# A two-layer hybrid decoder trunk on one core: the first layer's input loaded a second time by tokens, its loads put in order of use, products on ones while they run, and the feed-forward norm computed per token

## The chip, the core and the metric

The kernel runs on one core of a Trainium2 chip. TensorE (PE; its weight loads are listed as PEld) multiplies 128x128 stationary blocks with moving blocks of up to 512 columns into PSUM. VectorE (DVE), ScalarE (ACT) and GpSimd (POOL) do the elementwise work; SyncE (SP) and ACT issue DMAs. The metric is the device time in microseconds, the median of several runs; lower is better.

## The reference

```
def rmsnorm(x, g):
    y = xf * lax.rsqrt(jnp.mean(xf * xf, axis=-1, keepdims=True) + NORM_EPS)
    return (y * g.astype(jnp.float32)).astype(x.dtype)

def hybrid_layer(x, ...):
    h = rmsnorm(x, g_mix)
    z = h @ w_in                       # 1024 -> 2884 columns, split among the mixers
    y_a = short_conv_mixer(...)        # gated convolution, 3 taps
    y_b = gmlp_mixer(...)              # layernorm, 128x128 lower-triangular mixing
    y_c = dsa_mixer(...)               # rotary; indexer scores, top 128 keys, softmax
    y_d = conformer_conv_mixer(...)    # 31 taps, layernorm, silu
    x = x + jnp.concatenate([y_a, y_b, y_c, y_d], axis=-1) @ w_out
    hf = rmsnorm(x, g_ffn)
    return x + (jax.nn.silu(hf @ w_gate) * (hf @ w_up)) @ w_down
```

There are 512 tokens, a width of 1024, two such layers, a hidden width of 2816, and a last rmsnorm. Everything is float32.

## The kernel before

Channels lie on the 128 partitions and tokens along the row: x is eight tiles `X[k]` of 128x512. A float32 product is made from three products of two parts each: every operand is split into a rounded part (`hi`, fp32r, a cast on ACT) and the rest (`lo`, a subtraction on DVE or, for the weight units in `POOL_LO`, on POOL); `mm3` issues hi\*hi, hi\*lo and lo\*hi. Weights come in units of 128x1024 floats (512 KB) through three buffers `wr`; their halves go to four buffers each of `wh` and `wl`, or, for the units in `DEEP`, to the 68 general buffers `u`. A unit is 24 products of 512 columns (`unit`); its sum stands in one of three PSUM banks `mm` (a fourth, `cv`, is shared with the convolution).

A norm is not applied to x. The products run on x times its gain (`prep`, two instructions on ACT and DVE and a third for the squares), and the factor 1/rms of each token is multiplied in when a PSUM bank is read. So products can start before the norm's factor is known, but a bank can't be read and given free before it is.

Each layer: `proj("qi", 0)` (indexer queries), `proj("kw", 0)` (indexer keys and weights), then the other 21 input units, rotary, scores, the top-k search (`MAX8`, `MATCH_REPLACE8` on DVE), convolution taps on DVE (the first `TAPS[i]` of 31; the rest on ACT and POOL), attention, the output projection, and the feed-forward part. There, units alternate gate and up (`pgt`, `pu`); the gate's bank is multiplied by `R`, the row of factors, and only then is it free.

How the factors are made, in three places:

- First layer: `square_sum` squares each `X[k]` on ACT and sums over its partitions with four products of two columns on `ones` per tile (a stationary block of squares, `ones` moving), 32 in all, before any result; then `bank_rsqrt` on a 128x4 tile and `spread`, four products with the identity that put the factors of the four blocks of tokens across all partitions.
- Second layer and last norm: `square` adds up squares on POOL and DVE; `col_rsqrt` makes four products of two columns at the end; then the same.
- Feed-forward: `wide_rsqrt` (L638): sums by two products with `ones_r` that leave the sum in every partition, and then scale, reciprocal, square root and one Newton step on whole 128x512 tiles.

The order of instructions on every engine is made by a list scheduler in the program (`Program.order`). It has a planned cost per operation, a due time worked back from the end (`STRETCH`, `HURRY`), boosts per part of a layer (`BOOST`), a plan of TensorE's clock (`clock`) and of the DMA bus, and writes the instructions out in the planned order; on the chip each engine runs its list in that order and waits where it must. A change of one number or operation can so move instructions anywhere.

Of the kernel before, what the change touches and what calls it, by code (L numbers as in the profile page):

```python
# [113 lines left out]
class Op:  # L114
    __slots__ = ("eng", "cost", "lat", "fn", "tiles", "preds", "succs", "table", "late", "wait",
                 "ready", "main", "i", "dma", "start", "key", "boost", "desc", "port")
# [7 lines left out]
class Program:  # L124
# [15 lines left out]
    def add(self, eng, cost, fn, outs, ins, lat=LAT, table=None, main=False, dma=0.0,  # L140
            port=False):
        o = Op()
        o.port = port
# [24 lines left out]
    def order(self):  # L168
# [43 lines left out]
        table, bus, port, out, done = None, 0.0, 0.0, [], 0  # L212
        while done < len(ops):
# [65 lines left out]
            if e == "PE":  # L279
                end = self.clock(o.start, o.cost)  # L280
# [25 lines left out]
    def clock(self, start, cost):  # L306
# [7 lines left out]
        self.busy += self.slow * cost  # L314
        return start + self.slow * cost
# [6 lines left out]
    def mm(self, out, l, r, start, stop, main=False):  # L322
# [5 lines left out]
                 [out.tile.view], [l, r], lat=0.2, main=main)  # L328

# [24 lines left out]
    def tr(self, out, x, ident):  # L354
        self.add("PE", 0.109, lambda: self.nc.tensor.transpose(out.ap(), x.ap(), ident.ap()),
                 [out], [x, ident], lat=0.2)

# [80 lines left out]
HURRY = 1.19  # L438
# [5 lines left out]
    {"rope": -2.0, "conv": 19.0, "a": -4.0, "z": 2.0, "s": 12.0, "g": 6.0, "topk": -3.0, "att": 27.0, "out": -6.0},  # L444
    {"rope": 2.0, "conv": 26.0, "a": -1.0, "z": 0.0, "s": 6.0, "g": 0.0, "topk": 5.0, "att": 2.0, "out": 0.0},
]
DEEP = (4, 5, 6, 7, 9, 10, 11, 12, 13, 15, 23, 25, 31)
HALVED = (0,)
TAPS = (20, 20)
POOL_LO = (3, 5, 7, 10, 11, 12, 20, 21, 22, 23, 24, 25, 29, 30, 31, 32)  # L450
# [27 lines left out]
def _record(pg, nc, a, o, cst, sml):  # L478
# [24 lines left out]


    stream, gate = [0], []

    def weights():
# [48 lines left out]
    ones_r = const("ones_r", 128, F32R)  # L556
# [14 lines left out]
    def square_sum(k):  # L571

        sq = U()
        if k == 0:
            acc["pt"] = SM()
        pg.act(sq, X[k], AF.Square)
        for t in range(4):
            pg.mm(acc["pt"][:, 2 * t:2 * t + 2], sq[:, t * 128:(t + 1) * 128], ones[:, :2],
                  k == 0 and t == 0, k == KT - 1 and t == 3)

# [9 lines left out]
    def prep(k, l, col, sums=square):  # L590
# [4 lines left out]
        sums(k)  # L595
# [30 lines left out]
    def col_rsqrt(ss, scale, eps):  # L626
# [11 lines left out]
    def wide_rsqrt(ss, scale, eps):  # L638

        hi, lo, ms, r, y, t, R = U(F32R), U(F32R), U(), U(), U(), U(), U()  # L640
        split(ss, hi, lo)
        pt = SM()
        pg.mm(pt, ones_r, hi, True, False)
        pg.mm(pt, ones_r, lo, False, True)
        pg.ts(ms, pt, scale, eps, ALU.mult, ALU.add)
        recip(r, ms)
        pg.act(y, r, AF.Sqrt)
        pg.stt(t, y, -0.5, y, ALU.mult, ALU.mult)
        pg.tt(t, t, ms, ALU.mult)
        pg.stt(R, t, 1.5, y, ALU.add, ALU.mult)  # L650
        return R
# [10 lines left out]
    def layer(l, xg):  # L662
# [26 lines left out]
        def raw_of(pt):  # L689
# [3 lines left out]
            return pt, sw  # L693
# [5 lines left out]
        first = raw_of(first)  # L699
# [271 lines left out]
        R = wide_rsqrt(acc["ss"], 1.0 / D, 1e-6)  # L971
# [56 lines left out]
    pg.dma(prm[0], a["prm"][0])  # L1028
    for k in range(KT):
        pg.dma(X[k], a["x"][:, k], eng="ACT" if k % 2 else "SP")  # L1030
# [6 lines left out]
    pg.act(ones_r, ones)  # L1037
# [3 lines left out]
    xg = [prep(k, 0, P_GM, square_sum) for k in range(KT)]  # L1041
# [96 lines left out]
```

## Time and profile before

| | |
|---|---|
| runs | 1196.33 us median of 3 (1193.57 to 1197.22) |
| profiled execution | 1194.45 us, its span 1192.6 us |
| PE busy | 1156.8 us, 5278 instructions |
| DVE, ACT, POOL busy | 639.2, 483.8, 312.8 us |

The span runs from the first to the last instruction of the program; 1.85 us lie around it. A busy PE includes products that run at half the clock or are spaced out, so the number of products in a stretch says more than the busy time.

### The profile page before, as it was taken

The numbers are of one execution on the slowest core, as the hardware profiler recorded it, in microseconds if no ns is written. First come the engines' busy times: TensorE is split into PE (matmuls) and PEld (weight loads), VectorE is DVE, ScalarE is ACT, GpSimd is POOL, SyncE is SP. The second block draws the span as 40 slices with busy tenths as digits, with TensorE's granted clock in tenths as the row PEclk, the third lists the DMA queues.
The fourth block names the chain that finished last, engine by engine and source line by source line (L and its number), as shares of the span: only waits on it lengthen the run. The fifth ranks groups of instructions, "written<-read, shape, count | busy, mean of one in ns | idle before, by whom it ended". The sixth has DMA issues, their size and how long they took to land.

```text
span 1192.6 us, 13996 instructions
## 1 busy us (share of the span) xinstructions
PE 1156.8 (97%) x5278; PEld 942.5 (79%) x5278; DVE 639.2 (54%) x1126; ACT 483.8 (41%) x769; POOL 312.8 (26%) x236
## 2 busy tenths in 40 slices
PE   7999989989999999999999999998999999999996
PEld 7777867868888888888877788787888888888886
DVE  3589997754343434333257999868343434332222
ACT  6464558543333333232244563766232323222221
POOL 3516762311111111010044568323111111110001
PEclk9999999989999999999999999999999999999998
DMA  6630122222322232332255002222223232323322
GB/s 225 196 105 19 44 85 84 71 71 91 103 90 104 89 105 86 97 115 96 81 184 167 27 27 89 72 89 88 70 89 105 90 102 93 102 84 98 98 63 70
DMA packets 36547, 112.25 MB, mean 94 GB/s; under 512 B 4480, under 2 KB 6656, under 8 KB 36480
## 3 DMA queue, kind: packets, MB, share of 16 engines
q1 hardware_dynamic: 35904, 110.32, 28.5%
q10 hardware_dynamic: 576, 1.05, 0.3%
q8 instruction: 41, 0.67, 0.2%
q14 instruction: 26, 0.21, 0.1%
HBM read 105.06 MB, written 2.10 MB: 90 GB/s over the span
## 4 chain that ended last, share of the span: by engine, by line
PE 81%; DVE 12%; ACT 2%; DMA 2%; POOL 1%; issue 1%; DVEq 0%; POOLq 0%; ACTq 0%; SPq 0%
PE mm L326 75%; DVE u L366 3%; DVE u L897 3%; DVE m L896 2%; DVE cv L375 2%; PE sm L326 2%; PE sm L342 1%; DMA wr<-w_dram 1%; POOL u L366 1%; PE po L326 1%; DVE u L375 1%; DVE wl L366 1%; PE sm L351 1%; ACT u L414 1%; ACT u L412 1%
## 5 line engine op out<-in xcount | busy, mean ns | idle before, releaser
L326 PE MATMUL mm<-u,wh 128*128 128x512 f32 x2628 | 782.8, 393 | 10.7 <-DVE u L366 10.0
L326 PEld LDWEIGHTS mm<-u,wh 128*128 128x128 f32 x2628 | 493.8, 189 | 118.1 <-DVE u L366 11.1
L326 PE MATMUL mm<-u,wl 128*128 128x512 f32 x1314 | 467.4, 392 | 0.0
L366 POOL TENSOR_TENSOR u<-u,u 128x512 f32<-128x512 f32 (+11 forms) x170 | 229.7, 1360 | 708.9 <-ACT u L414 660.2
L412 ACT CAST wh<-wr 128x1024 fp32r<-128x1024 f32 (+3 forms) x174 | 173.7, 1008 | 465.4 <-PE mm L326 405.7
L326 PEld LDWEIGHTS mm<-u,wl 128*128 128x128 f32 x1314 | 247.5, 188 | 53.7 <-issue 1.7
L366 DVE TENSOR_TENSOR wl<-wr,wh 128x1024 fp32r<-128x1024 f32 (+2 forms) x158 | 186.6, 1182 | 143.2 <-ACT wh L412 135.1
L366 DVE TENSOR_TENSOR u<-mm,u 128x512 f32<-128x512 f32 x120 | 82.1, 689 | 280.4 <-PE mm L326 273.5
L326 PE MATMUL mm<-u,u 128*128 128x512 f32 (+1 forms) x696 | 180.7, 374 | 4.3 <-ACT u L412 3.2
L326 PEld LDWEIGHTS mm<-u,u 128*128 128x128 f32 x696 | 123.9, 188 | 32.7 <-ACT u L412 5.9
L412 ACT CAST u<-u 128x512 fp32r<-128x512 f32 (+1 forms) x84 | 49.0, 594 | 49.2 <-DVE u L366 33.4
L366 DVE TENSOR_TENSOR u<-u,u 128x512 fp32r<-128x512 f32 (+2 forms) x87 | 63.9, 746 | 5.6 <-ACT u L412 3.5
L366 DVE TENSOR_TENSOR X<-X,mm 128x512 f32<-128x512 f32 (+1 forms) x49 | 32.3, 671 | 46.6 <-PE mm L326 46.6
L375 DVE SCALAR_TENSOR_TENSOR cv<-u,prm,cv 128x511 f32<-128x511 f32 (+18 forms) x76 | 55.4, 729 | 0.0
L897 DVE MATCH_REPLACE8 u<-m,u 128x512 f32<-128x512 f32 (+2 forms) x96 | 51.5, 539 | 0.0
L896 DVE MAX8 m<-u 128x8 f32<-128x512 f32 (+2 forms) x96 | 51.0, 547 | 0.6 <-POOL u L564 0.5
L366 POOL TENSOR_TENSOR wl<-wr,wh 128x1024 fp32r<-128x1024 f32 (+1 forms) x16 | 36.0, 2253 | 54.3 <-ACT wh L412 50.1
L366 POOL TENSOR_TENSOR u<-wr,u 128x512 fp32r<-128x512 f32 (+1 forms) x32 | 41.3, 1309 | 24.8 <-ACT u L412 19.5
L412 ACT CAST u<-wr 128x512 fp32r<-128x512 f32 (+1 forms) x58 | 31.9, 601 | 31.7 <-DMA wr<-w_dram 31.0
L414 ACT ACTIVATE u<-u 128x512 f32<-128x512 f32 x54 | 34.1, 633 | 8.9 <-DVE u L366 5.5
L414 ACT ACTIVATE u<-X 128x512 f32<-128x512 f32 (+1 forms) x41 | 24.1, 609 | 30.9 <-DVE X L366 29.7
L414 ACT ACTIVATE u<-u,prm 128x512 f32<-128x512 f32 (+11 forms) x52 | 32.8, 706 | 7.2 <-POOL u L366 7.2
(99 smaller groups left out, 544.9 us busy)
## 6 DMA issues: line engine op xcount, KB each, us to landing
wr<-w_dram SPq DMA_DIRECT2D x167, 512.0 KB, 3.5
wr<-w_dram SPq DMA_DIRECT2D x32, 384.0 KB, 3.0
u<-u SPq DMA_DIRECT2D x28, 128.0 KB, 3.1
out_dram<-u SPq DMA_DIRECT2D x8, 256.0 KB, 2.6
X<-x_dram ACTq DMA_DIRECT2D x4, 256.0 KB, 5.2
X<-x_dram SPq DMA_DIRECT2D x4, 256.0 KB, 4.9
wr<-w_dram SPq DMA_DIRECT2D x2, 272.0 KB, 4.3
wr<-w_dram SPq DMA_DIRECT2D x2, 256.0 KB, 5.0
```

The costliest lines, as they stand in the source:

```text
L326: self.add("PE", cost, lambda: self.nc.tensor.matmul(out.ap(), l.ap(), r.ap(), start=start, stop=stop), [out.tile.view], [l, r], lat=0.2, ...
L342: self.nc.tensor.matmul(o.ap(), a.ap(), b.ap(), start=start, stop=stop)
L351: self.nc.tensor.transpose(o.ap(), x.ap(), ident.ap())
L366: self.add(eng, cost, lambda: self._e(eng).tensor_tensor(out=out.ap(), in0=a.ap(), in1=b.ap(), op=op), [out], [a, b], port=eng == "POOL" o ...
L375: self.add("DVE", 0.13 + 1.0417e-3 * out.n, lambda: self.nc.vector.scalar_tensor_tensor(out=out.ap(), in0=a.ap(), scalar=self._sc(s), in1= ...
L412: self.nc.scalar.copy(out.ap(), x.ap())
L414: self.nc.scalar.activation(out.ap(), x.ap(), func, **{k: self._sc(v) for k, v in kw.items()})
L896: pg.dve(n, lambda m8=m8, sc=sc: nc.vector.max(out=m8.ap(), in_=sc.ap()), [m8], [sc])
L897: pg.dve(n, lambda m8=m8, sc=sc: nc.vector.match_replace(out=sc.ap(), in_to_replace=m8.ap(), in_values=sc.ap(), imm_value=-3e38), [sc], [m8])
```

## The change

It has five parts. (1) x comes a second time, with tokens on the partitions (`xt`, eight tiles of 128x512, made on the host by a transposition of the input); in the first layer ACT squares these tiles with an accumulator that gives each token's sum, so `square_sum` and its 32 products are gone. (2) `first_load` gives the first loads a fixed rank: gains, `X[0]`, half of the first weight unit, `X[1]` and so on. (3) Twelve products of `ones` with itself (`warm`) stand at the head of PE's list. (4) The feed-forward norm is `rms()` (`col_rsqrt`, small tiles, and `spread`) in place of `wide_rsqrt`. (5) The scheduler's numbers: boosts, `HURRY`, a unit more in `DEEP`, two fewer in `POOL_LO`, `TAPS` 18 for the first convolution of each layer, no plan of heat for two-column products, and a bus that is busy for the first 3 us. In the first layer the first projection's bank is also copied out and freed before the factor is known (`free`).

```
-TAPS = (20, 20)
-POOL_LO = (3, 5, 7, 10, 11, 12, 20, 21, 22, 23, 24, 25, 29, 30, 31, 32)
+TAPS = (18, 20)
+POOL_LO = (5, 7, 10, 11, 12, 20, 21, 22, 23, 24, 25, 29, 31, 32)
-    {"rope": -2.0, "conv": 19.0, "a": -4.0, "z": 2.0, "s": 12.0, "g": 6.0, "topk": -3.0, "att": 27.0, "out": -6.0},
+    {"rope": -2.0, "conv": 19.0, "a": 16.0, "z": 2.0, "s": 30.0, "g": 4.0, "topk": 6.0, "att": 30.0, "out": 0.0},
...
+    def warm(self, out, x, n):
+        def fn():
+            for _ in range(n):
+                self.nc.tensor.matmul(out.ap(), x.ap(), x.ap(), start=True, stop=True)
...
+    def first_load(v, x, n, eng="SP"):
+        b, pg.boost = pg.boost, 2000.0 - 20 * n
+        pg.dma(v, x, eng=eng)
+        pg.boost = b
...
     def rms():
-        if "pt" in acc:
-            rs, pr = bank_rsqrt(acc.pop("pt"), 4, 1.0 / D, 1e-6)
+        if "xt" in acc:
+            ss, xt = small("ssq", 8), acc.pop("xt")
+            for i in range(8):
+                pg.act(xt[i], xt[i], AF.Square, acc=ss[:, i:i + 1])
+            st = small("sst", 4)
+            pg.tt(st, ss[:, :4], ss[:, 4:], ALU.add)
+            rs = rsqrt(st, 1.0 / D, 1e-6)
+            pr = spread(rs, 4)
...
+            if l == 0 and (name, i) == ("qi", 0):
+                pg.warm(pt[:, :128], ones, WARMUP)
...
-        R = wide_rsqrt(acc["ss"], 1.0 / D, 1e-6)
+        _, R = rms()
...
+    for k, (eng, n) in enumerate((("ACT", 1), ("ACT", 3), ("SP", 4), ("ACT", 5), ("SP", 6),
+                                  ("ACT", 7), ("SP", 9), ("SP", 10))):
+        first_load(X[k], a["x"][:, k], n, eng)
+    acc["xt"] = [U() for _ in range(8)]
+    for i, v in enumerate(acc["xt"]):
+        pg.dma(v, a["xt"][:, i])
```

What it moves, at three places. First, the head of PE's list, before (`sm` is the bank of the sums of squares, `u` a tile of squares or of x times gain, `wh` and `wl` the halves of the first weight unit):

```order
L326 MATMUL sm_128<-ones_86,u_122 128x2 x4
L326 MATMUL sm_128<-ones_86,u_116 128x2 x4
L326 MATMUL sm_128<-ones_86,u_158 128x2 x4
L326 MATMUL sm_128<-ones_86,u_130 128x2 x4
L326 MATMUL sm_128<-ones_86,u_177 128x2 x4
L326 MATMUL mm_199<-u_135,wh_183 128x512
L326 MATMUL mm_199<-u_145,wh_183 128x512
L326 MATMUL sm_128<-ones_86,u_194 128x2 x4
L326 MATMUL sm_128<-ones_86,u_201 128x2 x4
L326 MATMUL sm_128<-ones_86,u_209 128x2 x4
L326 MATMUL mm_199<-u_135,wl_190 128x512
L326 MATMUL mm_199<-u_142,wh_183 128x512
```

And after the change:

```order
L364 MATMUL mm_92<-ones_86 128x128 x12
L327 MATMUL mm_92<-u_135,wh_149 128x512
L327 MATMUL mm_92<-u_143,wh_149 128x512
L327 MATMUL mm_92<-u_135,wl_158 128x512
L327 MATMUL mm_92<-u_141,wh_149 128x512
L327 MATMUL mm_92<-u_151,wh_149 128x512
```

The sums are gone from between the unit's products. The `spread` of the factors (four products with `ident`) stood behind 24 products of 512 columns; it now stands behind 65.

Second, SP's queue of loads after the change, from the second half of the first weight unit on (`wr_127` is the second unit, `wr_155` the third; before, the third stood right behind the second):

```order
L432 DMA wr_109<-w_dram 128x512
L432 DMA X_123<-x_dram 128x512
L432 DMA X_125<-x_dram 128x512
L432 DMA wr_127<-w_dram 128x544
L432 DMA u_129<-xt_dram 128x512
L432 DMA u_131<-xt_dram 128x512
...
L432 DMA u_153<-xt_dram 128x512
L432 DMA wr_155<-w_dram 128x1024
L432 DMA ident_162<-ident_dram 128x128
L432 DMA cos_165<-cos_dram 128x512
```

The eight tiles of `xt` stand between the second and the third weight unit.

Third, the feed-forward norm of the first layer in DVE's list, before (`u_2318` is the sum of squares, `sm_2471` the bank of its sum over partitions, `u_2522` is `R`, `mm_2327` the first gate bank):

```order
L366 TENSOR_TENSOR u_2318<-u_2318,u_2446 128x512
L366 TENSOR_TENSOR u_2469<-u_2318,u_2462 128x512
L366 TENSOR_TENSOR wl_2476<-wr_2243,wh_2467 128x1024
L381 TENSOR_SCALAR u_2485<-sm_2471 128x512
L599 RECIPROCAL u_2492<-u_2485 128x512
L366 TENSOR_TENSOR wl_2509<-wr_2297,wh_2483 128x1024
L366 TENSOR_TENSOR wl_2513<-wr_2454,wh_2507 128x1024
L375 SCALAR_TENSOR_TENSOR u_2519<-u_2511 128x512
L366 TENSOR_TENSOR u_2519<-u_2519,u_2485 128x512
L375 SCALAR_TENSOR_TENSOR u_2522<-u_2519,u_2511 128x512
L366 TENSOR_TENSOR u_2524<-mm_2327,u_2522 128x512
```

And after the change (`sm_2442` is the bank of sums, `rs_2487` the factors, `u_2498` is `R`, `mm_2361` the first gate bank):

```order
L375 TENSOR_TENSOR u_2296<-u_2296,u_2414 128x512
L375 TENSOR_TENSOR wl_2438<-wr_2087,wh_2335 128x1024
L375 TENSOR_TENSOR wl_2448<-wr_2232,wh_2401 128x1024
L390 TENSOR_SCALAR sm_2442<-sm_2442 128x4
L375 TENSOR_TENSOR wl_2460<-wr_2276,wh_2440 128x1024
L605 RECIPROCAL rc_2469<-sm_2442 128x4
L384 SCALAR_TENSOR_TENSOR tt_2481<-sm_2442,tt_2481 128x4
L384 SCALAR_TENSOR_TENSOR rs_2487<-tt_2481,sm_2442 128x4
L375 TENSOR_TENSOR wl_2501<-wr_2451,wh_2490 128x1024
L375 TENSOR_TENSOR u_2508<-mm_2361,u_2498 128x512
```

The steps on 128x512 have become steps on 128x4. In PE's list 23 products of 512 columns stand between the four sums and the four products of the `spread` here, 18 in the second layer, and 11 in both layers between the `spread` and the first product that needs the gate's bank.

## Rows read from the trace of the kernel before

**Rows 1.** The page: span, and busy time by engine (share, instructions).

```profile
span 1192.6 us, 13996 instructions
PE 1156.8 (97%) x5278; PEld 942.5 (79%) x5278; DVE 639.2 (54%) x1126; ACT 483.8 (41%) x769; POOL 312.8 (26%) x236
```

**Rows 2.** Stretches: us, busy (x instructions) by engine, granted clock, DMA share, GB/s.

```profile
2.00:10.00 8.00, 3.46 (x17) 3.49 (x17) 2.44 (x4) 6.33 (x11) 0.00 (x0) 1.00 0.99 320
10.00:14.00 4.00, 4.00 (x20) 4.00 (x21) 3.59 (x6) 4.00 (x8) 0.00 (x0) 1.00 1.02 380
21.00:28.40 7.40, 7.40 (x22) 5.56 (x23) 2.03 (x5) 4.56 (x8) 4.19 (x3) 1.00 0.26 80
50.00:75.00 25.00, 24.32 (x111) 18.78 (x110) 15.46 (x24) 11.09 (x18) 5.05 (x5) 1.00 0.58 176
125.00:150.00 25.00, 25.00 (x112) 20.71 (x111) 25.00 (x60) 14.83 (x23) 19.85 (x14) 1.00 0.16 53
```

**Rows 3.** Timeline of the first 30 us: start, us, engine, what, wait before it.

```profile
0.80 1.87 ACTq L423 DMA_DIRECT2D X<-x_dram  x4
5.25 1.67 ACT L414 ACTIVATE u<-X 128x512 f32<-128x512 f32 x3 [0.96 <-DMA X<-x_dram]
6.54 8.68 PE L326 MATMUL sm<-ones,u 128*128 128x2 f32 x40 [6.54 <-ACT u L414]
15.09 1.20 PE L326 MATMUL mm<-u,wh 128*128 128x512 f32 x2
16.09 5.11 PE L326 MATMUL sm<-ones,u 128*128 128x2 f32 x24
21.06 0.77 PE L326 MATMUL mm<-u,wl 128*128 128x512 f32 x1
...
28.64 1.05 PE L326 MATMUL sm<-ident,rs 128*128 128x128 f32 x8
29.73 0.59 ACT L412 COPY u<-sm 128x512 f32<-128x512 f32 x1 [3.46 <-PE sm L326]
```

**Rows 4.** Chain that ended last: the first product of the indexer's scores.

```profile
66.75 0.90 PE sm L342 x6
```

**Rows 5.** Stretches of the two feed-forward starts and of the steady part behind them.

```profile
250.00:275.00 25.00, 19.20 (x77) 15.43 (x76) 13.49 (x15) 9.45 (x11) 3.13 (x3) 0.86 0.23 78
275.00:300.00 25.00, 25.00 (x112) 20.69 (x111) 8.67 (x10) 6.98 (x9) 4.24 (x3) 1.00 0.31 106
825.00:850.00 25.00, 21.46 (x83) 17.18 (x82) 12.84 (x15) 10.24 (x12) 2.52 (x2) 0.86 0.29 87
```

**Rows 6.** Timeline of the first layer's feed-forward start.

```profile
247.09 0.39 PE L326 MATMUL sm<-u,ones_r 128*128 128x512 f32 x1
248.85 3.35 DVE L599 RECIPROCAL u<-u 128x512 f32<-128x512 f32 x1
257.86 1.22 PE L326 MATMUL mm<-u,wh 128*128 128x512 f32 x2 [5.80 <-DVE u L366]
```

**Rows 7.** Timeline of the second layer's first norm.

```profile
611.46 0.95 PE L326 MATMUL sm<-ones,u 128*128 128x2 f32 x8
613.63 1.28 ACT L414 ACT_TABLE_LOAD   x1 [1.08 <-DVE rc L599]
615.94 0.16 DVE L375 SCALAR_TENSOR_TENSOR rs<-tt,sm 128x4 f32<-128x4 f32 x1
617.00 1.06 PE L326 MATMUL sm<-ident,rs 128*128 128x128 f32 x8
```

**Rows 8.** Groups by shape: busy us, mean ns of one, idle before.

```profile
L414 ACT ACTIVATE u<-X 128x512 f32<-128x512 f32 x39 | 23.3, 619 | 29.6 <-DVE X L366 28.7 <-DMA X<-x_dram 1.0
L414 ACT ACTIVATION_READ_ACCUMULATOR u<-u,mx 128x1 f32 x32 | 6.0, 188 | 0.0
L366 POOL TENSOR_TENSOR u<-u,u 128x491 f32<-128x491 f32 x4 | 5.1, 1271 | 8.2 <-ACT u L414 8.2
L375 DVE SCALAR_TENSOR_TENSOR cv<-u,prm,cv 128x494 f32<-128x494 f32 x4 | 2.9, 723 | 0.0
L366 DVE TENSOR_TENSOR wl<-wr,wh 128x1024 fp32r<-128x1024 f32 x133 | 163.4, 1229 | 68.2 <-ACT wh L412 60.2 <-PE mm L326 6.7 <-issue 1.3
```

More of the change, by code (lines that the diff above doesn't have):

```diff
@@ L115 @@
     __slots__ = ("eng", "cost", "lat", "fn", "tiles", "preds", "succs", "table", "late", "wait",
-                 "ready", "main", "i", "dma", "start", "key", "boost", "desc", "port")
+                 "ready", "main", "i", "dma", "start", "key", "boost", "desc", "port", "tiny")
 LAT = 0.14
@@ L211, in order @@
                 heapq.heappush(future[o.eng], (0.0, o.i))
-        table, bus, port, out, done = None, 0.0, 0.0, [], 0
+        table, bus, port, out, done = None, 3.0, 0.0, [], 0
         while done < len(ops):
@@ L279, in order @@
             if e == "PE":
-                end = self.clock(o.start, o.cost)
+                end = self.clock(o.start, o.cost, not o.tiny)
             if o.table:
@@ L304, in order, with clock @@
         return out
-    def clock(self, start, cost):
+    def clock(self, start, cost, heat=True):
         while start >= self.edge:
@@ L313, in clock @@
             self.edge, self.busy = self.edge + WINDOW, 0.0
-        self.busy += self.slow * cost
+        if heat:
+            self.busy += self.slow * cost
         return start + self.slow * cost
@@ L356, in tr @@
                  [out], [x, ident], lat=0.2)
+    def warm(self, out, x, n):
+        def fn():
+            for _ in range(n):
+                self.nc.tensor.matmul(out.ap(), x.ap(), x.ap(), start=True, stop=True)
+        self.add("PE", n * (1.667e-3 * out.n + 0.01), fn, [out], [x], lat=0.2)
     def _sc(self, s):
@@ L569, in _record @@
     acc = {}
[L571 to L579, printed above, removed]
     def square(k, c=slice(0, S)):
@@ L594, in prep @@
         pg.stt(xl, X[k], g, f(xh), ALU.mult, ALU.subtract)
-        sums(k)
+        if sums:
+            square(k)
         return xh, xl
@@ L692, in raw_of @@
             swap(raw, sw)
-            return pt, sw
+            return raw if free else pt, sw
         pg.boost = BOOST[l]["rope"]
@@ L698, in layer @@
         gate[:] = [next(o_ for o_ in pg.ops[n:] if o_.main)]
-        first = raw_of(first)
+        first = raw_of(first, l == 0)
         pk = proj("kw", 0)
@@ L1026, in finish @@
                 pg.dma(o[:, k:k + 2, c], t)
-    pg.dma(prm[0], a["prm"][0])
-    for k in range(KT):
-        pg.dma(X[k], a["x"][:, k], eng="ACT" if k % 2 else "SP")
+    first_load(prm[0], a["prm"][0], 0)
+    for k, (eng, n) in enumerate((("ACT", 1), ("ACT", 3), ("SP", 4), ("ACT", 5), ("SP", 6),
[4 more added lines that the diff above has]
+        pg.dma(v, a["xt"][:, i])
     pg.dma(ident, a["ident"])
@@ L1040, in _record @@
     select(caus, [[-1, 128]], -8e30, 1)
-    xg = [prep(k, 0, P_GM, square_sum) for k in range(KT)]
+    xg = [prep(k, 0, P_GM, False) for k in range(KT)]
     for l in range(L):
```

36 lines of the change are left out of this document (11 added, 25 removed).

## The prediction

> **What bounds the kernel now.** I read the page first, then stretches of 25 us, the waits, and the timeline of the places that stand out. PE is busy for 1156.8 of 1192.6 us [rows 1], but that includes slow and spaced products, so I count products: an undisturbed stretch has 112 of 512 columns in 25 us [rows 5], 0.2232 us each. What falls short of that rate is what a change of order and norms can win. Three places stand out.
>
> The start. The first x lands 4.4 us after its issue [rows 3]. Then PE does 64 rows of two-column products (each of the 32 runs as two) until 21.06, with two products of the first unit between them. The first unit really begins at 21.06, and only 22 products fit into the 7.4 us up to 28.40 [rows 2], 0.34 us each; in this stretch the spacing tells the clock, since the column for it reads 1.00. When the `spread` comes at 28.64, PE has done 24 of its useful products, which at the steady rate take 5.4 us.
>
> The two starts of the feed-forward part. In the first layer PE waits 5.80 us for DVE, which frees the gate's bank [rows 6]: between the product for the sum at 247.09 and the freed bank lie a reciprocal of 3.35 us and DVE's and ACT's other full-width steps. The granted clock then has a mean of 0.86 over 25 us, so part of them ran at 1.2 instead of 2.4 GHz, and only 77 products are done; in the second layer 83 [rows 5].
>
> The middle. From 25 to 75 us PE still does 111 instructions in 25 us; from 125 to 150 DVE is busy all the time and PE has its 112 [rows 2]. There both engines are near their limit, and I see no wait to remove.
>
> **The change part by part.** The sum is made against the profiled execution's 1194.45 us, which is 1.9 below the median of the runs.
>
> *Start.* First the loads. Gains, x and the first unit are 2.67 MB, the second unit 0.28, the second copy of x 2.10, the third unit 0.52. Before moves 320 GB/s from 2 to 10 us and 380 from 10 to 14 [rows 2], so 2.56 MB are in by 10.0 and 4.08 by 14.0. The last tile of x is then in at 10.3 us, the second unit at 11.1, the second copy at 16.6, the third unit at 18.0. One tile's way through ACT and DVE takes about 1.5 us with its waits, so the first unit's last products can run at about 12.3; until then PE follows the data. If it keeps up, 24 products (5.4 us) of the second unit are left at 12.3 to 12.5, and end at 17.8. The third unit waits for ACT, whose list has the eight squares of the second copy ahead of its cast: 0.62 us each and 0.19 to read the accumulator [rows 8], 6.5 us from about 12.4, so 18.9; the cast of 1024 columns ends at 20.0. 17 products and four small transpositions later PE is at the `spread`, at 24.4 us, with the factors ready at about 23. It has then done 65 products against 24 at 28.64: 41 x 0.2232 = 9.2 us, and 4.2 us earlier, in sum 13.4.
>
> That is the upper end. Two things lower it. The clock: the products on `ones` run while x is on its way and cost nothing (PE has nothing else to do before about 7 us; they would take twice 1.06 us for each four [rows 7], 6.4 in all, from 1.0 on). What they do to the clock no row shows: the two-column products ran from 6.54 to 21.2 without a pause, and still the first 22 products were slow. If it stays at 1.2 GHz until 17, PE does 21 products from 7.5 to 17 at twice 0.2232 us and the other 27 of its first two units by 23.0 instead of 17.8; the `spread` comes at 27.4, and 10.4 are left. And the factors: R comes at 24.4 + 1.06 + 0.59 = 26.1 instead of 30.32 [rows 3, 7], only 4.2 us earlier, and rotary and all later bank reads hang on it. If R, not the products, sets when the first scores come (66.75 [rows 4]), only 4.2 carry through. Between 4.2 and 13.4 I take **10**: PE is at the scores after almost the same work in both lists, and from 50 to 75 us it keeps its rate, so it is nearer to being the one that is waited for.
>
> *Feed-forward norm, both layers.* What can be won is 112 - 77 = 35 and 112 - 83 = 29 products [rows 5], 64 x 0.2232 = 14.3 us. What it costs PE: four sums of two columns (0.95 us) and a `spread` (1.06) [rows 7] less two products of 512 columns (0.45), 1.56 in each layer, 3.1 in all. Whether the wait is really gone: the small chain stands in the second layer's first norm, 4.48 us from the first sum to the factors with 1.08 of waiting in it [rows 7]. PE has the sums and 23 products ahead of the `spread` in the first layer (0.95 + 5.1 = 6.1 us) and 18 in the second (5.0), and 11 behind it (2.5 us) for the copy of R (0.59 [rows 3]) and one read of the bank on DVE (by the nearest row a tap, 0.72 [rows 8]). DVE also has a weight split of 1.23 us [rows 8] in both pieces. So it fits barely; I take 0.4 us of waiting in each layer, 0.8. Gain 14.3 - 3.1 - 0.8 = **10.4**. Bounds: all of the wait gone, 11.2; 3 us of it left in both layers, 5.2.
>
> *The rest.* The full-width steps that DVE loses (3.35 us of reciprocal and more) lie where DVE idles, once PE doesn't wait for them. Two taps less on DVE are 1.4 us off its full stretch and add 2.5 us to POOL's chain of taps [rows 8], which is covered as long as top-k search ends later than the convolution. The boosts reorder the full stretch with the same work in it. I take **0** for all of this, with 1.4 gained or 4 lost as its ends: should the cover fail, attention begins later by that much.
>
> Sum: 1194.45 - 10 - 10.4 = 1174.05, and I forecast **1174 us**, 1.9% under the median.
>
> A rule that speaks against the change: the Trainium skill ("DMA: Bandwidth & Descriptors", section "Issuing engines are not separate DMA queues") says that DMAs from whatever engine end up on the same 16 DMA engines and interleave, so that several queues save issue time alone. By it the second copy's 2.10 MB push back all that is loaded behind it, however it is queued, and the order of the loads only decides who waits; that is rival (d) below. The DMA share of 0.99 and 1.02 in [rows 2] agrees with it.
>
> **The rivals.** (a) *Nothing held back*: all 13.4 of the start, 11.2 of the norms and 1.4 of the taps: 1168. For it: PE waits little from 25 to 75 us. Against: the start then has to run at 2.4 GHz while the data come in pieces. (b) *R sets the pace*: 4.2 in place of 10, 1180. For it: rotary and every bank read need R. (c) *The factors come late for the `spread`*: PE works its list in order, so a late factor stops it with products behind it; 5.2 in place of 10.4, 1179. For it: the chain is 4.5 us and DVE has weight splits in it. Against: the lists leave 5.0 and 6.1. (d) *The second copy is paid in full*: its 2.10 MB at 380 GB/s, 5.5 us, come on top as the third unit is late: 1179.5. Against: by the reckoning above only about 2 us of it are bare. (e) *Slower*: the second copy arrives so late that R comes after the banks are full and PE stands. The place is PE's fourth unit. To lose what the norms win (10.4) and 3.6 more, R has to come at 30.3 + 14 = 44 us, which is 9.5 us after the copy is in by the reckoning above; the copy at about 35 instead of 16.6, its 2.10 MB from 11.1 on at 88 instead of 380 GB/s. No row of the first 14 us speaks for that. (f) *No change beyond 0.3%* (about what a measurement of this kernel can tell): (c) at its worst and (b) together with 4 us lost in the full stretch make 1189, still faster; it takes one more loss.
>
> **How the numbers follow.** Forecast, 1170 to 1178: 0.48. (a) 0.12. (b) 0.17. (c) 0.10. (d) 0.06. (e) 0.04. (f) 0.03. Faster by over 0.3% are all but (e) and (f): 0.93; the same 0.03; slower 0.04. The range reaches from 1165, which takes in most of (a), to 1186, which takes in (b), (c), (d) and a part of their sums.
>
> **What would show it.** Right: the `spread` of the first layer at 24 to 27 us; R's copy by 27; the first scores at 55 to 58; 105 or more products in each of the two 25 us stretches that hold a feed-forward start, with the clock at 1.00 there; no single wait of PE over 1 us after the first unit. Wrong in the start: a gap before the third unit, or products at twice 0.2232 us after 17 us. Wrong in the norm: PE waiting for DVE's factors at the `spread`. Wrong in the middle: more idle time of PE between 150 and 230 us than before, since the search or the convolution ends later.

## The result, and the profile after

The changed kernel takes 1176.41 us (median of 4 runs, 1175.02 to 1177.97), the kernel before 1196.68 in the same comparison: ratio 0.9836, 95% interval 0.9814 to 0.9858. The forecast was 1174, so time and sign came out as foretold, but the nearness is luck: the sum hides two errors that cancel, and one step that held only by the planner's new numbers.

The page of the changed kernel, against [rows 1]:

```profile
span 1173.8 us, 13981 instructions
PE 1147.5 (98%) x5266; PEld 936.3 (80%) x5266; DVE 630.0 (54%) x1123; ACT 483.4 (41%) x782; POOL 311.1 (27%) x238
```

The span is 18.8 us shorter. The start, as stretches (columns as in [rows 2]):

```profile
2.00:10.00 8.00, 6.45 (x29) 5.41 (x27) 3.41 (x6) 5.28 (x8) 0.00 (x0) 0.95 0.99 340
10.00:14.00 4.00, 4.00 (x14) 3.21 (x13) 3.91 (x7) 4.00 (x10) 0.00 (x0) 0.68 1.04 376
14.00:21.00 7.00, 7.00 (x32) 4.21 (x30) 0.91 (x4) 5.16 (x15) 0.64 (x1) 1.00 1.05 394
50.00:75.00 25.00, 25.00 (x119) 18.92 (x118) 22.90 (x48) 14.44 (x30) 5.61 (x6) 1.00 0.51 168
125.00:150.00 25.00, 24.52 (x107) 19.64 (x106) 25.00 (x62) 9.32 (x16) 23.83 (x19) 1.00 0.21 69
```

And as timeline, with the two longest waits of the middle behind it:

```profile
1.06 5.16 PE L364 MATMUL mm<-ones 128*128 128x128 f32 x24 [1.06 <-POOL ones L576]
7.58 0.73 PE L327 MATMUL mm<-u,wh 128*128 128x512 f32 x2 [1.36 <-ACT wh L421]
...
12.60 0.63 ACT L423 ACTIVATE u<-u 128x512 f32<-128x512 f32 x1
...
17.51 0.59 ACT L421 COPY u<-mm 128x512 f32<-128x512 f32 x1 [1.74 <-PE mm L327]
...
19.75 0.19 ACT L423 ACTIVATION_READ_ACCUMULATOR u<-u 128x1 f32 x1
...
25.73 1.05 PE L327 MATMUL sm<-ident,rs 128*128 128x128 f32 x8
...
26.82 0.59 ACT L421 COPY u<-sm 128x512 f32<-128x512 f32 x1 [0.83 <-PE sm L327]
...
157.63 0.79 PE L327 MATMUL mm<-u,u 128*128 128x512 f32 x1 [3.44 <-ACT u L421]
...
658.75 1.71 PE L344 MATMUL sm<-u,u 64*128 64x384 f32 x6 [3.15 <-ACT u L423]
```

The reader is to see that the first unit's products now begin at 7.58 us, not 21.06 (two stood alone at 15.09) [rows 3], while the data still come at 340 to 394 GB/s; that the `spread` stands at 25.73 instead of 28.64; and that there is a wait of over 3 us in the middle of each layer that the kernel before doesn't have (its longest there are 1.6 us between 140 and 240 us, and 1.1 between 610 and 810).

The feed-forward starts, against [rows 5]:

```profile
225.00:250.00 25.00, 25.00 (x120) 20.90 (x119) 15.14 (x20) 12.37 (x17) 5.99 (x5) 1.00 0.31 106
800.00:825.00 25.00, 25.00 (x119) 20.91 (x118) 14.96 (x20) 12.33 (x17) 6.64 (x5) 1.00 0.26 85
825.00:850.00 25.00, 25.00 (x112) 20.67 (x112) 10.91 (x13) 7.73 (x10) 3.19 (x2) 1.00 0.27 91
```

No wait, no fall of the clock, 119 or 120 matmuls where 77 and 83 stood (the small sums are among them). The chain that now makes the factors, against [rows 6]:

```profile
231.29 0.95 PE L327 MATMUL sm<-ones,u 128*128 128x2 f32 x8
...
233.77 0.17 DVE L605 RECIPROCAL rc<-sm 128x4 f32<-128x4 f32 x1
234.02 1.28 ACT L423 ACT_TABLE_LOAD   x1 [1.67 <-DVE rc L605]
...
235.93 0.16 DVE L384 SCALAR_TENSOR_TENSOR rs<-tt,sm 128x4 f32<-128x4 f32 x1
...
237.46 1.05 PE L327 MATMUL sm<-ident,rs 128*128 128x128 f32 x8
```

From the first sum to the factors are 4.8 us (235.93 + 0.16 - 231.29), and 1.4 us remain before the `spread`.

**Where the time went.** Marks such as "first scores" mislead when a list changes, since other work lies ahead of them. So I add up TensorE's products in the order in which they ran (columns divided by 512; two-column sums, products on `ones` and the `spread` of the layers' input and feed-forward norms left out; both kernels have 4892 such units) and ask in each trace when n units were begun. The lead over the kernel before is the difference:

```
units done (place in the kernel before)   before    after    lead
  24  first unit                            28.4     15.0    13.4
 250  search and convolution begin          82.1     68.3    13.8
 900  before the first feed-forward part   243.8    233.6    10.3
1000  behind its start                     275.0    257.2    17.8
2400  end of the first layer               592.4    574.5    17.8
3350  before the second feed-forward part  822.9    809.8    13.1
3400  behind its start                     840.8    822.1    18.7
4800  last down-projection                1158.2   1139.5    18.7
```

(Leads are taken before rounding.) Start +13.8, first middle -3.5, first norm +7.5, second layer's middle -4.7, second norm +5.6. This last column is used for every experiment below.

### The profile page after: what moved, and what is told of

Same layout as the page of the kernel before. It is cut to its first block, busy times and chain, and to the rows that moved or that the text cites. A ratio compares the mean times of both kernels' runs of the same rounds, so it can differ in the third digit from the quotient of the medians.

```text
span 1173.8 us, 13981 instructions
## 1 busy us (share of the span) xinstructions
PE 1147.5 (98%) x5266; PEld 936.3 (80%) x5266; DVE 630.0 (54%) x1123; ACT 483.4 (41%) x782; POOL 311.1 (27%) x238
## 3 DMA queue, kind: packets, MB, share of 16 engines
q10 hardware_dynamic: 576, 1.05, 0.3%
## 4 chain that ended last, share of the span: by engine, by line
PE 80%; DVE 12%; ACT 3%; POOL 2%; DMA 2%; issue 1%; SPq 0%; DVEq 0%; POOLq 0%; ACTq 0%
PE mm L327 75%; DVE cv L384 3%; DVE u L375 3%; DVE u L895 3%; DVE m L894 2%; POOL u L375 2%; PE sm L344 1%; PE po L327 1%; ACT u L423 1%; DVE u L384 1%; ACT u L421 1%; PE sm L353 1%; PE cv L327 1%; DMA u<-u 1%; DMA wr<-w_dram 1%
## 5 line engine op out<-in xcount | busy, mean ns | idle before, releaser
L327 PE MATMUL mm<-u,wh 128*128 128x512 f32 (+1 forms) x2596 | 769.6, 392 | 3.1 <-DVE u L375 1.7
L327 PEld LDWEIGHTS mm<-u,wh 128*128 128x128 f32 (+1 forms) x2596 | 485.5, 188 | 110.1 <-issue 4.0
L327 PE MATMUL mm<-u,wl 128*128 128x512 f32 (+1 forms) x1298 | 462.0, 392 | 0.4 <-DVE wl L375 0.2
L375 POOL TENSOR_TENSOR u<-u,u 128x512 f32<-128x512 f32 (+14 forms) x174 | 234.9, 1360 | 694.8 <-ACT u L423 650.2
L421 ACT CAST wh<-wr 128x1024 fp32r<-128x1024 f32 (+2 forms) x172 | 171.9, 1008 | 463.1 <-PE mm L327 405.3
L327 PEld LDWEIGHTS mm<-u,wl 128*128 128x128 f32 (+1 forms) x1298 | 243.5, 188 | 52.5 <-DVE wl L375 1.4
L375 DVE TENSOR_TENSOR wl<-wr,wh 128x1024 fp32r<-128x1024 f32 (+3 forms) x162 | 190.4, 1176 | 147.1 <-ACT wh L421 132.6
L384 DVE SCALAR_TENSOR_TENSOR cv<-u,prm,cv 128x511 f32<-128x511 f32 (+17 forms) x72 | 52.7, 732 | 0.1
L895 DVE MATCH_REPLACE8 u<-m,u 128x384 f32<-128x384 f32 (+2 forms) x96 | 51.5, 540 | 0.0
L894 DVE MAX8 m<-u 128x8 f32<-128x384 f32 (+2 forms) x96 | 50.7, 548 | 0.9 <-POOL u L579 0.8
L423 ACT ACTIVATE u<-u,prm 128x512 f32<-128x512 f32 (+13 forms) x56 | 36.0, 704 | 10.4 <-POOL u L375 9.7
L423 ACT ACTIVATE u<-X,prm 128x512 fp32r<-128x512 f32 (+1 forms) x39 | 27.2, 718 | 14.6 <-DVE X L375 14.2
```

The costliest lines, as they stand in the source:

```text
L327: self.add("PE", cost, lambda: self.nc.tensor.matmul(out.ap(), l.ap(), r.ap(), start=start, stop=stop), [out.tile.view], [l, r], lat=0.2, ...
L375: self.add(eng, cost, lambda: self._e(eng).tensor_tensor(out=out.ap(), in0=a.ap(), in1=b.ap(), op=op), [out], [a, b], port=eng == "POOL" o ...
L384: self.add("DVE", 0.13 + 1.0417e-3 * out.n, lambda: self.nc.vector.scalar_tensor_tensor(out=out.ap(), in0=a.ap(), scalar=self._sc(s), in1= ...
L421: self.nc.scalar.copy(out.ap(), x.ap())
L423: self.nc.scalar.activation(out.ap(), x.ap(), func, **{k: self._sc(v) for k, v in kw.items()})
L894: pg.dve(n, lambda m8=m8, sc=sc: nc.vector.max(out=m8.ap(), in_=sc.ap()), [m8], [sc])
```

## The experiments

First theory: start and norms give the gain as forecast, and the first layer's middle takes some back because VectorE sets the pace there (25.0 of 25 us busy), so that TensorE's lead beyond VectorE's is waited away. Rivals: TensorE sets the pace and the order of the lists puts the waits; or the planner's numbers make the gain or the loss. Each ratio below is to the kernel before on the same chip; the changed kernel's is 0.9836. Profiled spans stand beside 1173.8.

**1. Without the products on ones** (the order is kept).

```
         def fn():
-            for _ in range(n):
+            for _ in range(0):
                 self.nc.tensor.matmul(out.ap(), x.ap(), x.ap(), start=True, stop=True)
```

> The changed kernel without its twelve products on ones; every other instruction stands in the same order on its engine. Theory (they keep TensorE's clock up while x is under way, and cost nothing): the first unit runs at 1.2 GHz for longer, the second unit ends 2 to 4 us later than 20.6 us, and the kernel takes 1178 to 1180 us, since ACT's squares and the factors still set the spread at about 25.7 us and hide a part. Rival (the clock falls anyway while the data come in pieces, as it did between 9.15 and 12.57 us): 1176.4 us, within 1, and the granted clock of 2 to 14 us is hardly lower than now.

Measured: 1178.26 us, ratio 0.9856 (0.9834 to 0.9877), span 1173.6. 24 units are done at 15.4 us instead of 15.0, and the lead at the end is 18.6 instead of 18.7. The median lies in the theory's range, but 0.2% is within the intervals, so by the time neither is shown. The traces decide: the theory's 2 to 4 us of delay are 0.4. Without these products the first unit's products stand 0.43 us apart until 12.79 us and 0.23 behind it, which is half the clock and then the full one (the clock's column reads 1.00 there all the same, as in [rows 2]); with them the granted clock is 0.5 from 9.15 to 12.57 us. The clock that they bring is lost again when the first unit's data come in pieces (0.68 from 10 to 14 us above), before it has earned more than that.

**2 to 4. More on TensorE, more on VectorE, less on VectorE**, each in the first layer with the order kept. The second kernel does one product 16 times, the third two rounds' searches twice, the fourth leaves two rounds of sixteen out.

```
+        next(o for o in out if o.first and o.start > 80.0).more = 15
...
+                more = 2 if l == 0 and r in (2, 4) else 1
...
+                skip = l == 0 and r in (3, 5)
```

> The changed kernel with 15 more products of 128x512 on TensorE in the first layer, at about 80 us (the first product of a unit is done 16 times; the order is kept). By the steady spacing of 0.223 us they are 3.35 us of TensorE's time. Theory (from the first scores to the end of attention VectorE sets the pace of the first layer, and TensorE's lead beyond that is lost in waits): 1176.4 + 0 to 1.2 us, and the waits at 152 to 158 us are shorter by about 3. Rival (TensorE sets the pace, and the waits at 158 us come from where the planner put part s): 1176.4 + 3.3 = 1179.7 us.

> The changed kernel with six searches for the largest eight done twice in the first layer (two rounds of three blocks); the order is kept. By the spacing of such rows from 150 to 156 us (0.34, 0.47 and 0.60 us) that is 2.8 us more on VectorE. Theory (VectorE sets the pace of the first layer's middle): 1176.4 + 2.2 to 2.8 = 1178.6 to 1179.2 us. Rival (TensorE sets it): 1176.4 + 0 to 0.7 us.

> The changed kernel with two of the sixteen rounds of the top-k search left out in the first layer, so that it picks another number of keys there; the order of all else is kept. That takes 6.0 us off VectorE between 75 and 130 us (2.99 us a round by the spacing of the rows at 150 to 157 us). Theory (VectorE sets the pace and eats 4 of the 14.3 us that TensorE leads the kernel before by at 550 units of work): 3 to 5 us less, 1171.5 to 1173.5 us; at the first gate the lead over the kernel before is 13 to 15 us instead of 10.3. Rival (TensorE sets the pace, the waits are placed by the order): 1176.4 us, within 1.

Measured: more on TensorE 1181.00 us, 0.9883 (0.9864 to 0.9902), span 1176.1; more on VectorE 1179.33, 0.9870 (0.9850 to 0.9890), span 1179.3; less on VectorE 1175.82, 0.9835 (0.9815 to 0.9854), span 1174.1. The leads (the 15 extra products not counted as work):

```
units              250    900   1000   2400   3350   4800
changed kernel    13.8   10.3   17.8   17.8   13.1   18.7
more on TensorE   14.0    7.3   14.9   14.9   11.1   16.6
more on VectorE   13.7    7.3   14.8   14.8    7.8   13.4
less on VectorE   13.7   11.7   19.2   19.2   13.1   18.6
```

3.35 us on TensorE cost 2.9 at 1000 units, 2.8 us on VectorE cost 3.0, and 6.0 us off VectorE win 1.4, of which the median shows nothing. By the ratios the two additions cost more, 0.47% (5.6 us) and 0.34% (4.1 us); the profile with more on TensorE is of the fastest of its five runs. So the first theory falls: TensorE has no slack that its lead could be lost in. Nor is TensorE alone the pace, since VectorE's addition is paid in full too. With more on TensorE the wait looks like this:

```profile
160.63 0.80 PE L334 MATMUL mm<-u,u 128*128 128x512 f32 x1 [3.43 <-ACT u L429]
```

The same 3.4 us, 3.0 later: the wait isn't used up by a later TensorE. The lists of the engines are interlocked there (in the changed kernel VectorE waits 2.8 us at one place for a bank that TensorE fills, TensorE 2.7 us at three for tiles that VectorE makes), and a delay on either moves the whole.

**5. The two long waits filled with products**, seven on `ones` ahead of each, order kept. They write the bank that TensorE writes next (`sm324`, `sm1002`).

```
+        fill = {1341: sm["sm324"], 3766: sm["sm1002"]}
         for o in self.order():
+            for _ in range(7 if o.i in fill else 0):
+                self.nc.tensor.matmul(fill[o.i][:, :128].ap(), ones(), ones(), start=True, stop=True)
```

> The changed kernel with seven products of ones on ones (128x128, about 0.43 us each, 3.0 in all) ahead of each of the two longest waits, the one of 3.44 us at 157.63 us and the one of 3.15 us at 658.75; they use a bank that is written next anyway, and the order is kept. Theory (a wait in the middle costs twice: its own length, and the half clock behind it, granted from 155.92 to 162.75 and from 657.68 to 664.51 us): the clock stays at 1.00 in both places, some 2.5 us are won in the first layer and 2.9 in the second, in sum 1171 us; 1173 if VectorE's list takes back the half. Rival (the engines wait for one another there, and a faster TensorE only waits longer): 1176.4 us, within 1. Third: the products run over the end of the wait and cost 1 us at each place, 1178.

Measured: 1177.74 us, 0.9839 (0.9818 to 0.9860), span 1175.9. The timeline at both places:

```profile
153.80 1.72 PE L324 MATMUL sm<-ones 128*128 128x128 f32 x14
157.39 0.50 PE L332 MATMUL mm<-u,u 128*128 128x512 f32 x1 [1.86 <-ACT u L426]
...
660.12 3.31 PE L324 MATMUL sm<-ones 128*128 128x128 f32 x14 [3.15 <-ACT u L428]
```

In the first layer the fill lies in the wait. From 150 to 175 us the mean clock is 0.93 instead of 0.86, and still the lead is 10.5 against 10.3 at 900 units: nothing is won, as the rival said, for the product that waited goes no earlier (157.39, with everything 0.2 earlier since the start). The Trainium skill ("TensorE: Matmul & The Clock Gate", section "Loop structure matters more than you think") says that a long wait between matmuls takes their clock down and that matmuls back to back keep it up. The trace agrees as to the clock, which was half mended here, and no time came of it. In the second layer the experiment failed: the fill itself waited 3.15 us, as the bank that it was to write was what the scores wait for, and then ran ahead of them, so that they began at 663.36 instead of 658.75 us. It says nothing of what a higher clock would be worth there. The median is near the third expectation, but the loss is at the second place alone (the lead at the end is 16.4 instead of 18.7).

**6. The planner's old numbers** in the changed kernel.

```
-HURRY = 1.07
+HURRY = 1.19
...
-    {"rope": -2.0, "conv": 19.0, "a": 16.0, "z": 2.0, "s": 30.0, "g": 4.0, "topk": 6.0, "att": 30.0, "out": 0.0},
+    {"rope": -2.0, "conv": 19.0, "a": -4.0, "z": 2.0, "s": 12.0, "g": 6.0, "topk": -3.0, "att": 27.0, "out": -6.0},
```

(The second layer's boosts, DEEP, TAPS and POOL_LO are put back too; the plan's bus and heat and the early copy of the first bank stay as in the changed kernel.)

> The changed kernel with the planner's numbers of the kernel before (boosts, hurry, taps, deep units, units on POOL). Theory now (both engines are at their limit in the middle, and what is lost there is put there by the order): the start (spread at 25 to 27 us) and the two feed-forward starts stay as in the changed kernel, and the middles of both layers come out otherwise, by 5 to 12 us more, 1181 to 1188 us. Rival (the start and the norm alone carry the gain, the numbers are worth nothing): 1176.4 us, within 2. Second rival (the new numbers are what loses in the middle, 600 to 750 units of work): 1170 to 1174 us.

**9. One number put back**: the boost of the top-k search in the first layer.

```
-    {"rope": -2.0, "conv": 19.0, "a": 16.0, "z": 2.0, "s": 30.0, "g": 4.0, "topk": 6.0, "att": 30.0, "out": 0.0},
+    {"rope": -2.0, "conv": 19.0, "a": 16.0, "z": 2.0, "s": 30.0, "g": 4.0, "topk": -3.0, "att": 30.0, "out": 0.0},
```

> The changed kernel with one number put back: the boost of the top-k search in the first layer, 6 to -3. Theory (what the start wins is kept only if the search, which fills VectorE, also begins earlier; then attention and all behind it begin earlier): the start is as in the changed kernel up to 24 products at 15 us, the first search moves from 70 us to 85 us or more, the first step of attention from 171 us to 180 or later, and the first feed-forward part begins 8 us later or more: 1184 to 1195 us. Rival (the number moves work about in a stretch where the engines have the same work anyway, as the forecast held): 1176.4 us, within 2.

Measured: with the old numbers 1187.54 us, 0.9934 (0.9917 to 0.9951), span 1186.4; with one number put back 1203.95, 1.0083 (1.0069 to 1.0097), span 1202.4, slower than the kernel before.

```
units              24    250    900   1000   2400   3350   4800
changed kernel   13.4   13.8   10.3   17.8   17.8   13.1   18.7
old numbers      14.0   13.6   -1.4    1.4    1.4    0.7    6.3
one put back     14.5   13.9  -15.2   -8.6   -8.6  -15.8  -10.3
```

The start is won in all three and kept only in the first. The rows of the search show where it goes: the searches for the largest eight from 50 to 130 us (count, shortest, median and longest in ns, first and last start), the last striking out of eight found, and the first step of attention behind it on VectorE. The kernel before:

```profile
L896 DVE MAX8 m<-u x22: 401/610/687, 78.9 to 129.9; 128x8 f32<-128x512 f32 x11, 128x8 f32<-128x384 f32 x9, 128x8 f32<-128x256 f32 x2
...
181.98 0.40 DVE L897 MATCH_REPLACE8 u<-m,u 128x256 f32<-128x256 f32 x1
182.31 0.67 DVE L386 CUSTOM_DVE_ANT_0 u<-sm,u 128x512 f32<-128x512 f32 x1
```

The changed kernel:

```profile
L894 DVE MAX8 m<-u x26: 416/552/696, 70.2 to 129.0; 128x8 f32<-128x512 f32 x12, 128x8 f32<-128x384 f32 x11, 128x8 f32<-128x256 f32 x3
...
171.07 0.40 DVE L895 MATCH_REPLACE8 u<-m,u 128x256 f32<-128x256 f32 x1
171.40 0.67 DVE L395 CUSTOM_DVE_ANT_0 u<-sm,u 128x512 f32<-128x512 f32 x1
```

The old numbers:

```profile
L894 DVE MAX8 m<-u x17: 406/553/695, 96.7 to 127.0; 128x8 f32<-128x512 f32 x8, 128x8 f32<-128x384 f32 x6, 128x8 f32<-128x256 f32 x3
...
178.47 0.40 DVE L895 MATCH_REPLACE8 u<-m,u 128x256 f32<-128x256 f32 x1
...
182.81 0.69 DVE L395 CUSTOM_DVE_ANT_0 u<-sm,u 128x512 f32<-128x512 f32 x1
```

One number put back:

```profile
L894 DVE MAX8 m<-u x6: 548/692/697, 109.1 to 129.3; 128x8 f32<-128x512 f32 x4, 128x8 f32<-128x384 f32 x2
...
197.73 0.44 DVE L895 MATCH_REPLACE8 u<-m,u 128x256 f32<-128x256 f32 x1
198.06 0.71 DVE L395 CUSTOM_DVE_ANT_0 u<-sm,u 128x512 f32<-128x512 f32 x1
```

TensorE is 14 us ahead in all of the kernels with the new start, but with the old numbers the lists spend that on other units: 239 units are done before the first scores, 247 with the one number put back, 196 in the changed kernel, 182 in the kernel before. So the search begins at 96.7 us instead of 70.2 (78.9 in the kernel before). It ends earlier than in the kernel before even so, but other work of VectorE stands between it and attention, which begins at 182.8, where it began before the change (182.3; in the changed kernel 171.4). With the one number put back the search begins at 109.1 us and attention at 198.1. In both runs the lead stays up to 600 units (14.9 and 17.0 us) and is gone at 800 (-0.5 and -14.5). The rivals of both runs fall, and the second run is above the range of its own theory too. That the search alone is the cause isn't shown: the one number moves other instructions as well (the first scores come at 67.9 us instead of 56.5).

**7 and 8. The norm alone, and all but the norm.**

```
-        R = wide_rsqrt(acc["ss"], 1.0 / D, 1e-6)
+        _, R = rms()
```

in the kernel before, and the reverse in the changed kernel.

> The kernel before with the feed-forward norm per token alone; planner's numbers and start as before. Forecast's working: 10.4 us less than before, 1184. By the lead over the kernel before at the feed-forward starts of the changed kernel (7.5 us in the first layer, 5.6 in the second, counted by work done): 13.1 less, 1181 to 1182. Rival (the factors come late for the spread in these lists): 5.2 less, 1189. Another rival (what the norm wins was won because the start freed VectorE): nothing, 1195.

> The changed kernel with the full-width norm of the feed-forward part put back; start and planner's numbers as in the changed kernel. If the parts add up: 1176.4 + 10.4 to 13.1 = 1187 to 1189.5 us, and both feed-forward starts show the wait of about 5.8 us and the granted clock of 0.86 again. If the norm is worth less without its company: 1180 to 1184.

Measured: the norm alone 1187.60 us, 0.9932 (0.9913 to 0.9952), span 1186.0; all but the norm 1185.49, 0.9915 (0.9899 to 0.9932), span 1183.9. The gains of 0.68% and 0.85% add up to 1.53%, the whole change has 1.64%: within the intervals the parts add. Each alone lies between what the expectations gave for it: 8.1 us for the norm in the old lists, where 10.4, 13.1 and 5.2 stood, and 9.4 us for undoing it, where 10.4 to 13.1 or 3.6 to 7.6 stood. By the leads the norm alone wins 2.8 us in the first layer (-0.9 at 900 units, 1.9 at 1000) and 5.5 in the second (0.9 to 6.4); in the changed kernel, undoing it costs 5.8 and 5.7 (there the leads pass the two starts from 11.3 to 13.0 and from 8.8 to 8.7, with +7.5 and +5.6 in the changed kernel). First layer, norm alone in the old lists:

```profile
250.00:275.00 25.00, 23.12 (x100) 18.97 (x99) 9.54 (x13) 9.45 (x14) 4.08 (x3) 0.93 0.28 91
...
253.25 1.05 PE L326 MATMUL sm<-ident,rs 128*128 128x128 f32 x8
...
256.18 0.72 PE L326 MATMUL mm<-u,wh 128*128 128x512 f32 x2 [1.88 <-DVE u L366]
```

The factors aren't late (the `spread` runs without a wait), but the gate's bank is read late and the clock falls to a mean of 0.93. With all but the norm the old picture is back, though the wait is 3.54 us and not 5.80:

```profile
225.00:250.00 25.00, 21.45 (x81) 16.83 (x80) 19.37 (x21) 11.47 (x14) 4.13 (x4) 0.86 0.32 106
...
243.94 1.22 PE L327 MATMUL mm<-u,wh 128*128 128x512 f32 x2 [3.54 <-DVE u L375]
```

**10. Without the second copy of x**: its sums come from two-column products again.

```
+            pt = acc.pop("pt")
+            rs = rsqrt(pt[:, 0:8].fold(4)[:, :, 0], 1.0 / D, 1e-6, pt[:, 16:])
...
-    acc["xt"] = [U() for _ in range(8)]
...
+        else:
+            square_sum(k)
```

> The changed kernel without the second copy of x: the mean squares of the first layer come again from two-column products of the squares, which stand ahead of the first unit's products on TensorE. Order of the loads, warm products and numbers as in the changed kernel. Theory (most of the start's 13.4 us is these products, 64 rows of 0.11 to 0.22 us, off TensorE): 24 units of work are done at 20 to 24 us instead of 15.0 (28.4 in the kernel before), so 5 to 9 us of the start's lead are gone. What the lists behind it make of that in the middle is not foretold by the parts; if it goes through, 1181 to 1186 us. Rival (the order of the loads is what wins, and the sums hide behind the loads): 24 units at 15 to 17 us, and 1177 to 1179 us.

Measured: 1217.88 us, 1.0196 (1.0173 to 1.0219), span 1216.2.

```profile
10.78 10.40 PE L327 MATMUL sm<-ones,u 128*128 128x2 f32 x48 [0.60 <-ACT u L423]
...
26.99 1.16 PE L327 MATMUL sm<-ident,rs 128*128 128x128 f32 x8 [1.75 <-DVE rs L384]
```

48 rows of sums take 10.40 us; in the kernel before the 64 take 8.68 and 5.11 us [rows 3], 13.8 in sum, as much as the start's lead. 24 units are done at 30.1 us, later than in the kernel before (28.4): all of that lead hangs on these sums, more than the theory's 5 to 9, and the order of the loads by itself wins nothing while they stand there. The loss of 29.6 us by 900 units shows again what a start does that these numbers weren't made for (first search at 118.3 us); it is no measure of the second copy.

**11 and 12. Two other sets of numbers** for the changed kernel, for which its planner's own model ends earlier. The first set's first layer (the second layer, DEEP and POOL_LO change too):

```
-    {"rope": -2.0, "conv": 19.0, "a": 16.0, "z": 2.0, "s": 30.0, "g": 4.0, "topk": 6.0, "att": 30.0, "out": 0.0},
+    {"rope": 0.0, "conv": 19.0, "a": 16.0, "z": 2.0, "s": 24.0, "g": -4.0, "topk": 9.0, "att": 12.0, "out": 0.0},
```

> The changed kernel with other planner's numbers, for which its own planner's model of the engines ends 5 us earlier: search boost 9, part g -4, attention 12 in the first layer, one more deep unit, another list of units on POOL. Theory (the waits in the middle are put there by the order, and 8 us of the lead are lost there): some of the 8 come back, 1170 to 1175 us, and the waits of 3 us at 158 and 659 us are gone or shorter. Rival (the model of the planner doesn't see what the waits and the clock do, and each order loses about the same): 1175 to 1180 us.

> As the run before, with a second set: part s 14, attention 42, out -2 in the first layer, 17 taps on VectorE instead of 18 there, another list on POOL; the planner's model ends 2.5 us earlier than with the changed kernel's. Theory: 1172 to 1176 us. Rival: 1175 to 1180 us.

Measured: the first set 1173.89 us, 0.9828 (0.9813 to 0.9843), span 1173.2; the second 1180.36, 0.9888 (0.9873 to 0.9903), span 1176.6. The first keeps 14.6 us of lead at 900 units instead of 10.3, so the loss in the first middle is indeed put there by the order. But it loses 7.3 in the second layer (21.2 to 13.9) and ends with 19.5: its interval overlaps that of the changed kernel, and it isn't shown to be better. The wait at 158 us is gone (the longest between 60 and 250 us is 2.6), the one at 658 is still 3.2. The total doesn't decide: the median is in the theory's range, the ratio times 1196.68, 1176.1 us, in the rival's. The second set is slower than its theory says, and by the ratio (1183 us) than its rival too.

## Why the forecast came out, point by point

**Start: mechanism right, size low.** I took 10 between 4.2 and 13.4; the lead was 13.4 at 24 units and 13.8 at 250, the upper end. `spread` at 25.73 (forecast 24.4; 65 products done, as foretold), R's copy at 26.82 (26.1), first scores at 56.5 (55 to 58). What I held back for the clock and for R wasn't lost: the clock was low only from about 9 to 12.6 us, and rival (b), R as pace, falls, since R moved 2.9 us and the lead is 13.8 at 250 units. The first scores, my sign for it, are no measure: they moved 10.2 us by the new order, and with the old numbers they come at 66.1 though the lead at 250 units is 13.6. Rival (d) falls too: the DMA share is 0.99 to 1.05 until 21 us, and TensorE has its 65 products by 25.73 all the same. The products on `ones`, which I costed at nothing, show no gain either beyond 0.4 us at 24 units (run 1).

**Norms: mechanism right, size near.** 10.4 forecast; undoing them costs 9.4 us by the ratios (0.79%) and 11.5 by the leads. The lead's 13.1 at the two starts is above my bound of 11.2: the kernel before takes 31.2 us for 100 units at the first start and 17.9 for 50 at the second, 8.9 and 6.7 more than at the steady rate, where my two stretches of 25 us showed 14.3 in sum. Rival (c) had the right worry in the wrong place: in the old lists the factors are in time and the bank read behind them is late (run 7). The new lists leave no wait.

**The rest at 0: the step that failed.** It said that "the boosts reorder the full stretch with the same work in it". Measured were -3.5 us in the first middle and -4.7 in the second layer's, beyond my lower end of 4 together. (In runs 1 to 4, whose second layer has the same instructions in the same order, its middle loses 3.8 to 7.0 us: the sign is sure, the size isn't.) More than its size was wrong: the same work in another order moved the end by 12.6 us (run 6) and 28.6 (run 9) in the profiles. The start's gain isn't a term that adds to the others; it is a lead that the order of the lists carries to the attention or doesn't. My sum was near because the start and the norms by the leads were 3.8 and 2.7 us larger and the middles 8.2 worse (10 + 10.4 + 6.5 - 8.2 = 18.7), which is luck. Rival (a), nothing held back, had the start and the norms better than I (13.4 and 11.2), and it too lacked the loss in the middles.

**What was to show it.** The start and the starts of the feed-forward parts (119 and 120 matmuls, clock 1.00) came as written. "No single wait of PE over 1 us after the first unit" did not: 3.44 and 3.15 us. "Wrong in the middle" had the right sign and the wrong reason: PE idles 5.7 us between 150 and 230 us instead of 4.4, but the search ends earlier than before, by 10.9 us (its last step at 171.07 against 181.98), where it began 8.6 earlier.

**Open.** What takes 4.7 us in the second layer isn't settled. The wait at 658.75 is for a step of ACT (the read that frees the scores' bank, at 658.23) that stands behind a scaled tap, and that one behind POOL:

```profile
656.33 0.70 ACT L423 ACTIVATE u<-u,prm 128x483 f32<-128x483 f32 x1 [1.91 <-POOL u L375]
657.62 0.70 ACT L423 ACTIVATE u<-u,prm 128x482 f32<-128x482 f32 x1 [0.59 <-POOL u L375]
658.23 0.85 ACT L423 ACTIVATE u<-sm 128x384 f32<-128x384 f32 x2
```

The runs with the old lists (6 and 7) lose only 0.7 and 1.0 us between 2400 and 3350 units, so the new numbers take part in it; which of them does it was not tried. Nor were the order of the loads and the early copy of the first bank tried apart from the rest, and what makes the wait of 3.44 us in the first layer is known only so far that the first other set of numbers hasn't got it.

## What to carry to other kernels

Time won at the head of an interlocked program is a lead, not a saving: look for the longest chain on another engine that has to start from it (here the search on VectorE), and ask whether its beginning, its end and the step that waits for it move as well. Measure lead by work done on the engine that is busiest, at several places; marks and totals hide that one part gives back what another won. When a list planned ahead is tuned for one start, a part taken out alone says little of that part's worth.

## What was not expected of the hardware

With the same order of instructions, a wait of the same length lowers the granted clock in one run and not in another. In the second layer's first norm the changed kernel waits 2.13 us at 611.19 and keeps 1.00 from 600 to 625; in run 5, whose fill in the first layer lies far behind it, TensorE waits 2.12 us at 610.89 and the mean is 0.93, with 95 matmuls instead of 102 in that stretch; with more on VectorE it waits 2.75 us at 614.79, and the mean is 0.86. In this order:

```profile
600.00:625.00 25.00, 22.87 (x102) 18.63 (x102) 15.99 (x21) 11.29 (x19) 14.54 (x10) 1.00 0.70 215
611.19 0.73 PE L327 MATMUL mm<-wh,u 128*128 128x512 f32 x2 [2.13 <-ACT u L421]
...
600.00:625.00 25.00, 22.88 (x95) 18.45 (x94) 14.96 (x20) 10.86 (x19) 14.64 (x10) 0.93 0.69 210
610.89 0.72 PE L332 MATMUL mm<-wh,u 128*128 128x512 f32 x2 [2.12 <-ACT u L426]
...
600.00:625.00 25.00, 22.25 (x91) 17.76 (x90) 14.34 (x19) 10.93 (x20) 16.61 (x12) 0.86 0.71 219
614.79 1.22 PE L327 MATMUL mm<-wh,u 128*128 128x512 f32 x2 [2.75 <-ACT u L421]
```

The length of the wait alone doesn't decide it: run 1 waits 2.37 us there and keeps 1.00. What does isn't shown. From 2400 to 2600 units the run with more on VectorE loses 3.4 us against the changed kernel without a changed instruction there, more than the 2.8 that were added in the first layer. Differences of 2 or 3 us between single profiles of such kernels can be this alone, those between the second layers above among them.
